# Layer 1's softmax join written one step later, V's products three steps behind the scores, and the last head's share of the output projection kept apart

## The chip, the cores and the metric

The kernel runs on one core of a Trainium2 chip. The metric is the device time of one execution in microseconds. The engines are called as in the profile: PE (TensorE, matrix products), DVE (VectorE), ACT (ScalarE), POOL (GpSimd), SP (SyncE, which here only issues DMAs).

## What is computed

The reference is a two-layer backbone over 1024 latent tokens (`x`, 1024 wide) and 256 context tokens, batch 1. Layer 0 is multi-head latent attention, layer 1 is differential attention. Both kernels compute layer 0 in the same way; the change lies in layer 1, where the context tokens serve as keys and values alone:

```python
def diff_mixer(h, h_c, rows, need_ctx, layer_idx, w_in, lam, g_sub):
    ...
    lam_full = jnp.exp(jnp.sum(lam[0] * lam[1])) - jnp.exp(jnp.sum(lam[2] * lam[3])) + lambda_init
    q, k, v, gate = project(h, True)              # 8 heads, two q/k pairs of 64 each, v of 128, rotary on q and k
    q_c, k_c, v_c, gate_c = project(h_c, False)
    o1, o1_c = prefix_attention(q[:, :, :, 0:1], k[:, :, :, 0], v, ...)   # softmax over 1024 + 256 keys
    o2, o2_c = prefix_attention(q[:, :, :, 1:2], k[:, :, :, 1], v, ...)
    o = o1 - lam_full * o2
    o = rms_norm(o, g_sub) * (1.0 - lambda_init)
    return gated(o, gate)                          # o * silu(gate)
...
x = layer_norm(DEEPNORM_ALPHA * x + gate[:, None, :] * (o @ out_w[i]), ln_g[i], ln_b[i])
```

## The kernel before

All of layer 1 is cut into steps (h, t): head h of eight, tile t of eight with 128 query tokens each. In the profile it runs from about 1020 us to the end. Products that need more than half precision are made as three matmuls of high and low halves (`mm3`, lines L187 to L189). All PSUM banks (eight of 512 floats) are taken in turn under one name, `ps_b`.

A step of head h does the following, on the engines named:

- Scores (`scores1`): PE makes the scores of tile t against 1280 keys for both softmaxes m = 0, 1 (L1147, L1148; tiles `KS`, `QS`, `Q1`), the 256 context keys of both first. DVE takes the maxima (L1160, L1164, joined in L1166, L1169; tile `mx`), ACT the six exponentials with their sums (L1172, into `p0`, `p1` and `sm`).
- Join: DVE adds the sums (L1175), takes reciprocals (L1176), forms the factor of the second softmax (L1177) and makes `p0 + factor * p1` (L1178, 128x1280). After that V needs one product instead of two.
- Turn (`turn1`): ACT rounds the joined probabilities to half precision (L1184), POOL takes the rest (L1185), SP issues a DMA that transposes both halves into `pT` (L1187).
- Values (`values1`): PE multiplies `pT` by V's halves `vh`, `vl` in 30 matmuls (L1194 to L1196), ACT scales the result (L1199) and sums its squares (L1200), POOL takes the power for the norm (`rstd_of`, L161, L162) and scales (L1207), SP stores the 128x128 tile to `o_d` in DRAM (L1208). In the last head DVE multiplies by the gate instead and writes into the output tile (L1205).

Between these pieces PE works on a second stream, the projections of the next head (`prod_k1`, `prod_q1`, `prod_v1`) and the scaled weights of the one after (`prod_w`): K and Q are projected, rotated by DVE and POOL (`rope1`, L1051 to L1054, tiles `rsw`, `kr`, `rr`), scaled and split by ACT and DVE (L183 to L184, `kH`, `kL`), and put in place by DMAs. V and the gate come out of one projection, and ACT copies them to `Vf` and `gg` (L1125, L1127). The parts of the second stream are cut into slots by the table `SLOT1` through the function `some`, which takes pieces until their cost is used up.

The values of a step are taken two steps later: `turned` holds what is waiting. Tiles come from rotating pools: `p0` and `p1` two buffers each, `pT` two, `sm` four. A tile that is taken again waits until the readers of the one before are through.

In the last head the second stream is the output projection instead. `out_open` gives the projection's memory free, loads the layer norm's rows (`gb2`, `gb3`), loads the stored output of seven heads and the gate for tile 0 (`out_load`, POOL multiplies them in L1264), and loads, scales and splits the last four of the eight weight blocks (`out_w1`, DVE, L1235 and L179). From step 2 on, step t transposes the gated output of tile t-1 (`out_turns`, PE L1276, halves `tH`, `tL` by ACT L178 and DVE L179) and multiplies tile t-2 by the weights, its last 128 columns being transposed and multiplied at the end (`out_tile1`). The layer norm follows: DVE adds and takes statistics (L1311, L1312, L1315), POOL, ACT and POOL finish (L161, L162, L1325 to L1328), SP stores. Tile 7 ends with DVE (L1320, L1321).

PE's instructions stand in the order in which the code is written. DVE, ACT, POOL and SP are put in order by a scheduler, which goes by its own costs; so a line that is written elsewhere can stand on these engines where it stood, or not.

## Time and profile before

| | |
|---|---|
| median of three runs | 1881.55 us (1880.38 to 1882.77) |
| the profiled execution | 1876.05 us, its span 1874.3 us |
| busy in the span | PE 88%, DVE 64%, ACT 56%, POOL 55% |
| mean clock granted to PE | 0.951 of full speed |
| layer 1, heads 0 to 6 | 1020 to 1691.4 us |
| layer 1, last head | 1691.4 to 1874.3 us |

The profile shows one execution. Its instructions carry the line of the kernel, the engine, the tiles by name (buffer numbers left out) and the shape; a wait names what ended it. The busy time of PE includes the fill of its array, and while PE's granted clock is below 1 its instructions take longer. In a list of waits the columns after the names are the sum in us, the count and the longest.

### The profile page before, as it was taken

The page shows a single profiled execution, that of the slowest core. Times are in us where ns is not written, and L with a number is a line of the kernel's source. Part 1 is how long each engine was busy: PE and PEld are TensorE (multiplying, and loading weights), DVE is VectorE, ACT ScalarE, POOL GpSimd, SP SyncE. Part 2 cuts the span into 40 slices and gives each one's busy share as a digit, 9 for nine tenths or more (in the row PEclk, how much of TensorE's full clock was granted, in tenths as well). Part 3 has the DMA queues.
Part 4 walks back from the last instruction along what each step waited for, and adds up shares of the span by engine and source line. Part 5 has one row for each costly group of instructions (what it writes and reads, how often), then busy time and mean ns, then how long its engine had stood idle before and what let it go on. Part 6 is the DMA issues. An engine that isn't in the chain of part 4 may idle for free. (4 is left out here: it accounts for less than half of the span.)

```text
span 1874.3 us, 35281 instructions
## 1 busy us (share of the span) xinstructions
PE 1648.6 (88%) x13828; PEld 1179.7 (63%) x13828; DVE 1192.5 (64%) x1947; ACT 1058.0 (56%) x2017; POOL 1025.5 (55%) x801
## 2 busy tenths in 40 slices
PE   7889989999999998878879988988888898883997
PEld 3889965656666665556657564756475656462766
DVE  7545765565665657436754867686867686767463
ACT  3432157877777788701124666676666676765442
POOL 1443036767777676746652546464646465665565
PEclk8999899999999999989989999999999899997999
DMA  8245630110111113053333445555454455446553
GB/s 294 73 128 185 185 106 18 39 46 23 40 44 38 29 43 110 17 202 112 112 127 111 115 105 120 116 119 121 106 112 102 107 114 111 109 86 180 147 147 98
DMA packets 277108, 196.71 MB, mean 105 GB/s; under 512 B 179303, under 2 KB 250567, under 8 KB 276942
## 3 DMA queue, kind: packets, MB, share of 16 engines
q1 hardware_dynamic: 270126, 188.17, 38.2%
q10 hardware_dynamic: 6816, 6.29, 1.0%
q8 instruction: 108, 1.77, 0.4%
q14 instruction: 58, 0.48, 0.1%
HBM read 98.65 MB, written 27.07 MB: 67 GB/s over the span
## 5 line engine op out<-in xcount | busy, mean ns | idle before, releaser
L718 POOL TENSOR_TENSOR pl<-p,ph 128x1024 f16<-128x1024 f32 (+1 forms) x176 | 363.8, 2072 | 149.0 <-ACT ph L717 122.5
L1172 ACT ACTIVATE p<-ps_b,mx 128x512 f32<-128x512 f32 (+1 forms) x384 | 231.0, 620 | 65.9 <-DVE mx L1169 53.9
L716 ACT ACTIVATE p<-ps_a,esc 128x1024 f32<-128x1024 f32 (+1 forms) x176 | 189.2, 1075 | 96.0 <-PE ps_a L774 89.5
L698 DVE TENSOR_REDUCE mx<-ps_a 128x1 f32<-128x1024 f32 x128 | 155.5, 1223 | 134.8 <-PE ps_a L696 134.8
L1185 POOL TENSOR_TENSOR p<-p,p 128x1280 f16<-128x1280 f32 x64 | 169.4, 2647 | 73.0 <-ACT p L1184 72.8
L717 ACT CAST ph<-p 128x1024 f16<-128x1024 f32 (+1 forms) x176 | 177.1, 1006 | 5.5
L1194 PE MATMUL ps_b<-vh,pT 128*128 128x128 f16 x640 | 120.8, 230 | 60.6 <-DMA pT<-p 59.9
L1164 DVE TENSOR_REDUCE mx<-ps_b 128x1 f32<-128x512 f32 x256 | 167.8, 680 | 3.2 <-PE ps_b L1148 3.1
L187 PE MATMUL ps_b<-wH,h1H 128*128 128x256 f16 x512 | 145.3, 284 | 16.5 <-ACT p L1172 16.5
L1147 PE MATMUL ps_b<-KS,QS 128*128 128x512 f16 (+1 forms) x384 | 129.0, 351 | 33.2 <-ACT p L1172 29.4
L787 PE MATMUL ps_d<-Vh,pl 128*128 128x65 f16 x1344 | 145.9, 194 | 6.7 <-POOL pl L718 6.7
L784 PE MATMUL ps_d<-Vh,ph 128*128 128x65 f16 x1344 | 148.0, 195 | 0.0
L786 PE MATMUL ps_d<-Vl,ph 128*128 128x64 f16 x1344 | 146.8, 193 | 0.0
L188 PE MATMUL ps_b<-wL,h1H 128*128 128x256 f16 x512 | 145.1, 283 | 0.0
L189 PE MATMUL ps_b<-wH,h1L 128*128 128x256 f16 x512 | 144.7, 283 | 0.0
L187 PE MATMUL ps_b<-h1H,wH 128*128 128x512 f16 (+1 forms) x384 | 135.3, 352 | 6.3 <-ACT wH L183 6.2
L189 PE MATMUL ps_b<-h1H,wL 128*128 128x512 f16 (+1 forms) x384 | 134.5, 350 | 0.7 <-DVE wL L184 0.7
L188 PE MATMUL ps_b<-h1L,wH 128*128 128x512 f16 (+1 forms) x384 | 134.9, 351 | 0.0
L784 PEld LDWEIGHTS <-ph 128*128 128x128 f16 x1344 | 123.2, 97 | 18.1 <-issue 4.8
L1184 ACT CAST p<-p 128x1280 f16<-128x1280 f32 x64 | 80.4, 1257 | 92.5 <-DVE p L1178 77.6
L1148 PE MATMUL ps_b<-KS,Q 128*128 128x512 f16 (+1 forms) x384 | 131.6, 352 | 0.0
L786 PEld LDWEIGHTS <-ph 128*128 128x128 f16 x1344 | 123.9, 98 | 12.0
(370 smaller groups left out, 5012.1 us busy)
## 6 DMA issues: line engine op xcount, KB each, us to landing
ws<-in_dw SPq DMA_DIRECT2D x30, 512.0 KB, 5.1
adw<-in_ada_w SPq DMA_DIRECT2D x24, 512.0 KB, 4.8
g<-sg_d SPq DMA_DIRECT2D x18, 512.0 KB, 3.9
adaw<-in_ada_w SPq DMA_DIRECT2D x16, 512.0 KB, 6.9
sg_d<-gg ACTq DMA_DIRECT2D x40, 128.0 KB, 3.3
o<-o_d SPq DMA_DIRECT2D x10, 512.0 KB, 3.5
o_d<-op SPq DMA_DIRECT2D x7, 640.0 KB, 3.3
xt<-in_xT SPq DMA_DIRECT2D x16, 256.0 KB, 3.6
```

The source lines that it names most:

```text
L187: pe.matmul(ps, aH, bH, start=start, stop=False, skip_group_check=skip)
L188: pe.matmul(ps, aH, bL, start=False, stop=False, skip_group_check=skip)
L189: pe.matmul(ps, aL, bH, start=False, stop=stop, skip_group_check=skip)
L698: dve.tensor_reduce(mx[:, t, 0:1], ps, axis=AX.X, op=ALU.max)
L716: act.activation(p32[:, :n], st, AF.Exp, scale=esc0)
L717: act.copy(ph[:, :n], p32[:, :n])
L718: pool.tensor_tensor(pl[:, :n], p32[:, :n], ph[:, :n], op=ALU.subtract)
L784: pe.matmul(pv[:, t, :], ph[:, ts], Vh[:, k, h, :], start=(k == kcs[0] and t == 0), stop=False, skip_group_check=True)
L786: pe.matmul(pv[:, t, :V0], ph[:, ts], Vl[:, k, h, :], start=False, stop=False, skip_group_check=True)
L1164: dve.tensor_reduce(mx[:, 2 + 2 * m + i:3 + 2 * m + i], b, axis=AX.X, op=ALU.max, negate=True)
L1172: act.activation(p[m][:, c0:c0 + n], b, AF.Exp, bias=nb, accum_out=sm[:, 2 + 3 * m + i:3 + 3 * m + i])
L1185: pool.tensor_tensor(hl[:, 1, :], p0, hl[:, 0, :], op=ALU.subtract)
```

## The change

In heads 0 to 6 the join, the rounding and the subtraction become a function `join1`, which is written in the next step, between the scores of m = 0 and the first slot. The DMA that transposes is issued at the end of that step. Values are taken three steps behind the scores (`keep` is 2), after the second slot instead of ahead of it; from step (6,7) on two steps behind. For this a third buffer `pTx` takes every third tile. It lies where `Vf` lay, and V's float copy now uses K's tile `kr`. The stores to `o_d` are put on a list `late` and issued at the end of the step.

In the last head, the output of seven heads is 896 columns wide, and the last head's share has tiles of its own (`o7`, `g7`). `out_main(t-1)` multiplies the seven blocks in step t, `out_fin(t-2)` transposes the eighth, multiplies it into banks of its own and adds them on DVE, which makes two more additions per tile. The table `FIN` says where these pieces stand between those of `out_main`. The rows of the layer norm are loaded at the end of step 1, the four weight blocks through four `z` buffers. Scores and values of the last head stand in steps 0 to 9, the table `VO` says in which slot values stand, and the stores of the output are issued a step later.

The core of the diff (the renamed parts and the tables of the tiles are cut):

```diff
+FIN = 2, 4, 7, 10
+VO = 0, 2, 0, 0, 0, 0, 0, 0, 0, 0
...
-            "Vf": ([P, NT, P], F32, 1), "cosB": ([P, SEQ], F32, 1),
+            "pTx": ([P, 2 * NT, P], F16, 1), "cosB": ([P, SEQ], F32, 1),
...
-        gg, Vf = w1("gg"), w1("Vf")
...
-            yield
+            yield p, sm
+
+    def join1(h, t, p, sm):
...
-        yield turn1(*p), sm
-
-    def turn1(p0, p1):
-
-        hl = p1.bitcast(F16).rearrange("p (a b) -> p a b", a=2)
-        act.copy(hl[:, 0, :], p0)
-        pool.tensor_tensor(hl[:, 1, :], p0, hl[:, 0, :], op=ALU.subtract)
-        pT = w1("pT")
-        sp.dma_start_transpose(pT, hl.rearrange("p a b -> p (a b)"))
-        return pT
+        hl = p[1].bitcast(F16).rearrange("p (a b) -> p a b", a=2)
+        act.copy(hl[:, 0, :], p[0])
+        pool.tensor_tensor(hl[:, 1, :], p[0], hl[:, 0, :], op=ALU.subtract)
+        nT[0] += 1
+        pT = w1("pTx" if nT[0] % 3 == 0 and (h, t) < (H1 - 2, 5) else "pT")
+        turned.append((h, t, pT, sm))
+        return lambda: sp.dma_start_transpose(pT, hl.rearrange("p a b -> p (a b)"))
...
-            dve.scalar_tensor_tensor(oo[:, c], o, ss[:, 1:2], g[:, c], op0=ALU.mult, op1=ALU.mult)
+            o7[t] = w1("o7")
+            dve.scalar_tensor_tensor(o7[t], o, ss[:, 1:2], og[t][1], op0=ALU.mult, op1=ALU.mult)
...
-        sp.dma_start(o_d[1][t * P:(t + 1) * P, h * P:(h + 1) * P], o)
...
+        late.append((step[0], lambda: sp.dma_start(o_d[1][t * P:(t + 1) * P, h * P:(h + 1) * P], o)))
...
+        rest = [big.tile([P, 5, D], F32R, tag=tg, name=nm("o1")) for tg in ("bigA", "bigB")]
+        oHL.extend([r[:, k - NOW, :] for r in rest] for k in range(NOW, KT))
+        out_load(0)
+
+    def out_ws(*ks):
+        for k in ks:
+            for _ in out_w1(k, lambda: w1("z")):
+                pass
+
+    def out_gb():
         for tag, src in (("gb2", ln_g), ("gb3", ln_b)):
             og[tag] = w1(tag)
             bcast_row(og[tag], src[1:2, :])
-        rest = [big.tile([P, 5, D], F32R, tag=tg, name=nm("o1")) for tg in ("bigA", "bigB")]
-        oHL.extend([r[:, k - NOW, :] for r in rest] for k in range(NOW, KT))
-        out_load(0)
-        for k in range(NOW, KT):
-            z = [w1("z"), w1("res")][k % 2]
-            for _ in out_w1(k, lambda: z):
-                pass
-            if k == NOW:
-                out_load(1)
...
+        o, g, g7 = w1("o"), w1("g"), w1("g7")
+        og[t] = o, g7
+        sp.dma_start(o, o_d[1][ts, :DH])
+        sp.dma_start(g, sg_d[1][ts, :DH])
+        sp.dma_start(g7, sg_d[1][ts, DH:])
+        pool.tensor_tensor(o, o, g, op=ALU.mult)
...
+    def out_main(t):
+
+        z = zs[t] = w1("z")
+        sp.dma_start(z, zn_d[t * P:(t + 1) * P, :])
+        y = [bank("b") for _ in range(2)]
+        for k0, k1 in ((0, 4), (4, KT - 1)):
+            for hh in range(2):
+                for k in range(k0, k1):
+                    out_mm(y, t, hh, k, 0, KT - 2)
+                    yield 1600
+                if k1 == KT - 1:
+                    c = slice(hh * 512, hh * 512 + 512)
+                    dve.tensor_tensor(z[:, c], y[hh], z[:, c], op=ALU.add)
+
+    def out_fin(t):
         ts = slice(t * P, (t + 1) * P)
+        out_turn(t, KT - 1, 1)
+        yield 256
+        z, bs = zs.pop(t), w1("bs")
         y = [bank("b") for _ in range(2)]
+        for hh in range(2):
+            out_mm(y, t, hh, KT - 1, KT - 1, KT - 1)
             c = slice(hh * 512, hh * 512 + 512)
+            dve.tensor_tensor(z[:, c], y[hh], z[:, c], op=ALU.add)
             dve.bn_stats(bs[:, hh, :], z[:, c])
...
+        late.append((step[0] + 1, lambda: sp.dma_start(out[ts, :], z)))
...
+        def step1(cur, side, at, vpos=1):
+
+            if cur:
+                S = scores1(*cur)
+                pq = next(S)
+            turn = None
+            keep = 2 if cur and cur < (H1 - 2, SEQ // P - 1) else 1 if joined else 0
+            if joined:
+                turn = join1(*joined.pop(0))
             some(side, at[0])
+            if cur:
+                next(S)
+                joined.append((*cur, *pq))
+            for i, v in enumerate(at[1:]):
+                if i == vpos:
+                    while len(turned) > keep:
+                        values1(*turned.pop(0))
                 some(side, v)
+            if turn:
+                turn()
+            while late and late[0][0] <= step[0]:
+                late.pop(0)[1]()
+            step[0] += 1
...
+        out_open()
+        n = SEQ // P
+        for t in range(n + 2):
+            if t == 0:
+                out_ws(4, 5)
+                G = iter(())
+            else:
+                if t == 1:
+                    out_ws(6, 7)
+                    out_load(1)
+                if t < n - 1:
+                    out_load(t + 1)
+                if t == 1:
+                    late.append((step[0], out_gb))
+                if t < n:
+                    G = weave(out_main(t - 1), chain(out_turns(t), out_fin(t - 2) if t >= 2 else ()),
+                              FIN if t >= 2 else (9, 12))
+                    if t == 1:
+                        G = chain(out_turns(0), G)
+                elif t == n:
+                    F = out_fin(t - 2)
+                    G = weave(out_main(t - 1), (v for _, v in zip(range(1), F)), (7,))
+                else:
+                    G = chain(F, out_fin(t - 2))
             credit[0] = 0
+            step1((H1 - 1, t) if t < n else None, G, SLOTO, VO[t])
```

How this moves instructions is shown at three places. The first is DVE in head 5, from the end of step 2 to step 3: L1175 to L1178 (after: L1182 to L1185) are the join of tile 2, L1160 and L1164 (after: L1164, L1168) the maxima of tile 3, L184 (L186) the low halves of K and Q, L1051 and L1052 (L1055, L1056) the rotation of Q. Before:

```order
L184 SCALAR_TENSOR_TENSOR kL_19006<-kr_18619,kc_92,kH_19005 128x1280
L1175 TENSOR_REDUCE sm_18868<-sm_18868 128x2
L1051 STREAM_SHUFFLE rsw_18981<-ps_b_18899 128x512
L1052 TENSOR_TENSOR rr_18980<-ps_b_18899,cosB_12236 128x512
L1176 RECIPROCAL sm_18868<-sm_18868 128x2
L1160 TENSOR_REDUCE mx_19025<-ps_b_19029 128x2
L1177 SCALAR_TENSOR_TENSOR sm_18868<-sm_18868,nlam 128x1
L1164 TENSOR_REDUCE mx_19025<-ps_b_19035 128x1
L1178 SCALAR_TENSOR_TENSOR p_2803_18869<-p_2804_18870,sm_18868,p_2803_18869 128x1280
L1164 TENSOR_REDUCE mx_19025<-ps_b_19054 128x1
L184 SCALAR_TENSOR_TENSOR kL_19014<-rr_18980,es_18283,kH_19013 128x512
```

The rotation, the low half of K and the first maxima stand inside the join. After:

```order
L1182 TENSOR_REDUCE sm_18819<-sm_18819 128x2
L1183 RECIPROCAL sm_18819<-sm_18819 128x2
L1184 SCALAR_TENSOR_TENSOR sm_18819<-sm_18819,nlam 128x1
L1185 SCALAR_TENSOR_TENSOR p_2798_18820<-p_2799_18821,sm_18819,p_2798_18820 128x1280
L1055 STREAM_SHUFFLE rsw_18938<-ps_b_18857 128x512
L1056 TENSOR_TENSOR rr_18937<-ps_b_18857,cosB_12236 128x512
L186 SCALAR_TENSOR_TENSOR kL_18957<-kr_18577,kc_92,kH_18956 128x1280
L1164 TENSOR_REDUCE mx_18976<-ps_b_18980 128x2
L1168 TENSOR_REDUCE mx_18976<-ps_b_18986 128x1
L1168 TENSOR_REDUCE mx_18976<-ps_b_18990 128x1
```

The four parts of the join now stand together, ahead of the rotation, the low half of K and all maxima of tile 3; the low half of Q has gone behind these.

The second place is DVE at the opening of the last head: L1235 and L179 (after: L1237, L181) scale the weight blocks (`z`, `res`) and take their low halves, L1178 (L1185) are joins, `tL` is the low half of the transposed output of tile 0, for which PE's first products of the output wait. Before:

```order
L1178 SCALAR_TENSOR_TENSOR p_3131_21065<-p_3132_21066,sm_21064,p_3131_21065 128x1280
L1235 SCALAR_TENSOR_TENSOR z_20950<-z_20950,gsub,gate_12249 128x1024
L1178 SCALAR_TENSOR_TENSOR p_3117_20981<-p_3118_20982,sm_20980,p_3117_20981 128x1280
L179 TENSOR_TENSOR o_3102_20944<-z_20950,o_3101_20943 128x1024
L1235 SCALAR_TENSOR_TENSOR res_20962<-res_20962,gsub,gate_12249 128x1024
L1166 TENSOR_SCALAR mx_21152<-mx_21152 128x1
L1164 TENSOR_REDUCE mx_21152<-ps_b_21162 128x1
L1235 SCALAR_TENSOR_TENSOR z_20967<-z_20967,gsub,gate_12249 128x1024
L179 TENSOR_TENSOR o_3102_20944<-res_20962,o_3101_20943 128x1024
L1235 SCALAR_TENSOR_TENSOR res_20974<-res_20974,gsub,gate_12249 128x1024
L179 TENSOR_TENSOR o_3102_20944<-z_20967,o_3101_20943 128x1024
```

The join of tile 1 stands ahead of that of tile 0, and the weights follow with the maxima of tile 2 between them. After:

```order
L1185 SCALAR_TENSOR_TENSOR p_3107_20952<-p_3108_20953,sm_20951,p_3107_20952 128x1280
L1237 SCALAR_TENSOR_TENSOR z_20940<-z_20940,gsub,gate_12249 128x1024
L1182 TENSOR_REDUCE sm_21059<-sm_21059 128x2
L1237 SCALAR_TENSOR_TENSOR z_20945<-z_20945,gsub,gate_12249 128x1024
L181 TENSOR_TENSOR o_3099_20932<-z_20940,o_3098_20931 128x1024
L1237 SCALAR_TENSOR_TENSOR z_21034<-z_21034,gsub,gate_12249 128x1024
L181 TENSOR_TENSOR o_3099_20932<-z_20945,o_3098_20931 128x1024
L1237 SCALAR_TENSOR_TENSOR z_21039<-z_21039,gsub,gate_12249 128x1024
L181 TENSOR_TENSOR o_3099_20932<-z_21034,o_3098_20931 128x1024
L181 TENSOR_TENSOR tL_21101<-ps_b_21102,tH_21100 128x512
L181 TENSOR_TENSOR o_3099_20932<-z_21039,o_3098_20931 128x1024
L181 TENSOR_TENSOR tL_21101<-ps_b_21109,tH_21100 128x384
```

The four scalings and three low halves now stand behind the join of tile 0 and ahead of the first `tL`; the join of tile 1 comes after both parts of `tL`.

The third place is POOL at the very end: L1327 and L1328 (after: L1341, L1342) are the layer norm's products and sums of tile 6, the powers of `mv` belong to the layer norm and those of `ss` to the attention's norm of tile 7. Before:

```order
L161 TENSOR_SCALAR mv_22323<-mv_22323 128x1
L162 TENSOR_TENSOR mv_22323<-mv_22323,neghalf 128x1
L1325 TENSOR_SCALAR mv_22323<-mv_22323 128x1
L161 TENSOR_SCALAR ss_22365<-ss_22365 128x1
L162 TENSOR_TENSOR ss_22365<-ss_22365,neghalf 128x1
L1327 TENSOR_TENSOR z_22311<-z_22311,gb_3099_20939 128x1024
L1328 TENSOR_TENSOR z_22311<-z_22311,gb_3100_20941 128x1024
L161 TENSOR_SCALAR mv_22434<-mv_22434 128x1
L162 TENSOR_TENSOR mv_22434<-mv_22434,neghalf 128x1
```

The power of tile 7's attention norm stands ahead of tile 6's products, that of its layer norm behind them, with the whole of tile 7's products on PE between the two. After:

```order
L163 TENSOR_SCALAR ss_22431<-ss_22431 128x1
L164 TENSOR_TENSOR ss_22431<-ss_22431,neghalf 128x1
L163 TENSOR_SCALAR mv_22452<-mv_22452 128x1
L164 TENSOR_TENSOR mv_22452<-mv_22452,neghalf 128x1
L1339 TENSOR_SCALAR mv_22452<-mv_22452 128x1
L1341 TENSOR_TENSOR z_22206<-z_22206,gb_3152_21219 128x1024
L163 TENSOR_SCALAR mv_22477<-mv_22477 128x1
L1342 TENSOR_TENSOR z_22206<-z_22206,gb_3153_21221 128x1024
L164 TENSOR_TENSOR mv_22477<-mv_22477,neghalf 128x1
```

Now the two norms of tile 7 stand closer to each other, and tile 6's products are between them, the last one directly ahead of the last power.

More of the change, by code (lines that the diff above doesn't have):

```diff
@@ L1241, in out_open @@
         prj.close()
+        opened.append(1)
         wo = a1.enter_context(spool("a1out"))
@@ L1398, in hybrid_kernel @@
             for _ in G:
                 pass
-        for t in range(SEQ // P - 2, SEQ // P):
-            G = weave(out_tile1(t), out_turns(t + 1), (9, 12))
+        while later:
+            later.pop(0)()
+        out_open()
[22 more added lines that the diff above has]
+                    G = chain(F, out_fin(t - 2))
```

97 lines of the change are left out of this document (24 added, 73 removed).

## The prediction

> **What bounds the kernel now.** I read the page first, then the stretches of layer 1 (heads 0 to 6 run from 1020 to 1691.4 us, the last head from there to the end), then the waits of each engine in them, then single rows. Layer 0 and the set-up run the same instructions in both kernels, so everything before 1020 us is left as it is.
>
> ```profile
> PE 1648.6 (88%) x13828; PEld 1179.7 (63%) x13828; DVE 1192.5 (64%) x1947; ACT 1058.0 (56%) x2017; POOL 1025.5 (55%) x801
> ...
> 1020.00:1691.40 671.40, 590.10 (x4730) 409.42 (x4729) 480.10 (x912) 446.78 (x1157) 363.91 (x364) 0.95 0.50 111
> 1691.40:1733.25 41.85, 12.76 (x99) 8.54 (x97) 34.27 (x42) 21.98 (x43) 22.64 (x16) 0.68 0.59 184
> 1733.25:1865.00 131.75, 125.22 (x746) 96.74 (x747) 62.89 (x131) 52.47 (x133) 75.55 (x69) 0.99 0.50 136
> ```
>
> The columns after the length are the busy times of PE, PEld, DVE, ACT and POOL, then PE's granted clock. PE is the fullest engine, and in heads 0 to 6 it stands still for 671.4 - 590.1 = 81 us. These are its waits there:
>
> ```profile
> PE ps_b L1194 <- DMA pT<-p: 34.9, 19, 3.7
> PE ps_b L1147 <- ACT p L1172: 26.1, 23, 4.6
> PE ps_b L187 <- ACT p L1172: 16.5, 6, 3.7
> ```
>
> The first is V's product waiting for the transposed probabilities, which the third pT buffer and the longer lag are made to remove. The others wait for a PSUM bank that the exponentials still read. Whether the 34.9 us are worth 34.9 us is the question, and two whole heads answer it (4, then 5, each with PE's wait for pT):
>
> ```profile
> 1404.70:1500.90 96.20, 85.40 (x685) 58.75 (x683) 68.05 (x131) 65.09 (x169) 52.93 (x54) 0.95 0.49 106
> PE ps_b L1194 <- DMA pT<-p: 0.6, 1, 0.6
> ...
> 1500.90:1593.20 92.30, 82.51 (x681) 57.66 (x679) 67.25 (x128) 62.19 (x157) 53.71 (x53) 0.96 0.53 111
> PE ps_b L1194 <- DMA pT<-p: 6.2, 3, 2.2
> ```
>
> Head 4 is nearly free of this wait and takes 96.2 us; head 5 waits 6.2 us and takes 92.3. The wait is not what makes a head long: where PE doesn't wait for pT, it waits for a bank a little later. Who waits for whom on the other side:
>
> ```profile
> DVE sm L1175 <- ACT p L1172: 112.9, 43, 3.7
> DVE mx L1160 <- PE ps_b L1148: 1.4, 3, 0.8
> ...
> ACT p L1172 <- DVE mx L1169: 53.9, 23, 4.8
> ACT p L1184 <- DVE p L1178: 49.5, 42, 3.5
> ```
>
> DVE waits 112.9 us for the exponentials (L1175 is the first instruction of the join) and 1.4 us for the context's scores; ACT waits 103.4 us for DVE. So a chain bounds the heads: maxima, six exponentials, join, the next maxima. PE follows it.
>
> **The change, part by part.** *Heads 0 to 6.* Written one step later, the join could go behind the next step's maxima and open that chain. On DVE it hardly does: in most steps the sum still stands ahead of the next step's maxima, waiting for the same six exponentials. What is left are small moves, priced by these rows of head 5 (mean ns behind the comma):
>
> ```profile
> L1164 DVE TENSOR_REDUCE mx<-ps_b 128x1 f32<-128x512 f32 x32 | 20.9, 679 | 0.0
> L1178 DVE SCALAR_TENSOR_TENSOR p<-p,sm,p 128x1280 f32<-128x1280 f32 x8 | 13.5, 1685 | 0.3
> ...
> L184 DVE SCALAR_TENSOR_TENSOR kL<-kr,kc,kH 128x1280 f16<-128x1280 f32 x1 | 1.5, 1543 | 0.0
> L184 DVE SCALAR_TENSOR_TENSOR kL<-rr,es,kH 128x512 f16<-128x512 f32 x2 | 1.5, 743 | 1.7 <-DMA Q<-kL 1.7
> L1052 DVE TENSOR_TENSOR rr<-ps_b,cosB 128x512 f32<-128x512 f32 x2 | 1.3, 672 | 0.0
> ...
> L288 DVE TENSOR_SCALAR uw<-uw 128x1 f32<-128x1 f32 x2 | 0.3, 144 | 0.0
> ```
>
> - Join 2 leaves its place behind the low half of K (1.54), the two operations of a rotation (0.67 each at least) and two maxima (1.36): it ends about 4.2 us earlier. This takes most of the pT wait of steps 4 and 5. The next maxima have the same work ahead of them as before, less one low half of Q (0.74): exponentials 3 start about 0.7 us earlier.
> - In step 4 the first three exponentials no longer have a low half of Q (0.74) and a join (1.69) ahead of them on DVE, but a maximum (0.68) moves behind the sum of step 3: up to 1.75 us earlier for three of the six, nothing for the others. I take half, 0.9.
> - In step 6 of four heads the weights' scales (six operations like L288, 0.15 each) go ahead of the maxima: 0.9 us later, 0.5 as a mean over the heads.
> - In step 5 two operations of that size move behind the maxima: 0.3 us earlier.
>
> Together -0.7 - 0.9 + 0.5 - 0.3 = -1.4 us per head, times seven: **-10 us**. The bounds are +0.9 x 7 = +6 (only the delay comes through) and -48 (first rival). PE's freed pT waits are otherwise taken over by the bank waits. The third buffer and V's float copy in `kr` add no instruction; the copies into `kr` need K's halves to be read, which ACT and DVE do two steps earlier, and K's next rotation needs vl, which stands ahead of it on DVE in both kernels. The o_d stores, now issued at a step's end, leave SP free for the transposition; nobody waits for them before the last head.
>
> *Opening of the last head.* Today PE has its longest hole here, from 1708.3 to 1733.25:
>
> ```profile
> PE ps_b L1194 <- DMA pT<-p: 24.9, 1, 24.9
> ...
> SPq L1187 <- POOL p L1185: 17.5, 1, 17.5
> ...
> 1712.06 2.67 DVE L1235 SCALAR_TENSOR_TENSOR z<-z,gsub,gate 128x1024 f32<-128x1024 f32 x1 [0.34 <-issue]
> ...
> 1716.12 1.21 DVE L179 TENSOR_TENSOR o<-z,o 128x1024 fp32r<-128x1024 f32 x1
> 1717.25 1.27 DVE L1235 SCALAR_TENSOR_TENSOR res<-res,gsub,gate 128x1024 f32<-128x1024 f32 x1
> ...
> 1719.23 3.43 DVE L1235 SCALAR_TENSOR_TENSOR z<-z,gsub,gate 128x1024 f32<-128x1024 f32 x1
> 1722.58 3.10 DVE L179 TENSOR_TENSOR o<-res,o 128x1024 fp32r<-128x1024 f32 x1
> ```
>
> SP's transposition waits 17.5 us for POOL, whose order puts tile 1 ahead of tile 0. After the change that transposition isn't the next thing PE needs: it goes to the transposes of tile 0's output and its first products. These need tL, and DVE has four scalings and three low halves of the weights ahead of tL. Starting at 1712.06, 20.7 us into the head, they take 4 x 1.27 + 3 x 1.21 = 8.7 us undisturbed and 4 x 3.43 + 3 x 3.10 = 23 at the slowest rows. The new stretch has one subtraction of POOL less beside it than today's, in which about half of the rows are slow, so I add a third of the difference, 5. PE gets on at 20.7 + 13.7 = 34 us (ends 30 and 44) where it took 41.85. The Trainium skill, "SBUF — State Buffer", section "Who interferes with whom", says that a DVE instruction with two SBUF inputs is blocked by a GpSimd instruction that reads SBUF, for its whole length; by that each of POOL's operations there (a subtraction of 2.6 us and two products of 2.1) would cost DVE its full time: an estimate of 36 us and a sum 2 us higher. The rows of 1.27 and 3.43 agree with it.
>
> *Steps of the last head.* From the hole's end to PE's end 125.2 us are busy. Of that fall away 1.3 (its clock of 0.99), tile 0's seven transposes (done before, under 1) and 3.1 (the last 12 products, now behind V's last product, 0.26 each); 2.2 (scores of tile 2) and 1.7 (V's product of (6,7)) come in from before the hole: 124 us. The prices are from these rows, the starts of the last scores, of V's product after them, of the output's first product and of the third after it:
>
> ```profile
> 1821.52 0.28 PE L1147 MATMUL ps_b<-KS,QS 128*128 128x256 f16 x1
> ...
> 1823.69 0.22 PE L1194 MATMUL ps_b<-vh,pT 128*128 128x128 f16 x1
> ...
> 1825.34 0.48 PE L187 MATMUL ps_b<-oH,tH 128*128 128x512 f32 x1
> ...
> 1826.12 0.40 PE L187 MATMUL ps_b<-oH,tH 128*128 128x512 f32 x1
> ...
> PE ps_b L187 <- ACT tH L178: 6.1, 6, 1.3
> ```
>
> The 6.1 us of waits for tH go, since tile t's products now come a step behind its transposes; the k=7 transposes behind each V product bring new ones for o7, whose norm shares POOL with the layer norm. I take 4 us, ends 0 and 14.
>
> *Tail.* Now V's last product is followed by nearly the whole norm, the last 12 products and the layer norm:
>
> ```profile
> 1854.57 0.37 ACT L1199 ACTIVATE o<-ps_b,sm 128x128 f32<-128x128 f32 x1 [3.96 <-PE ps_b L1196]
> ...
> 1855.10 0.19 POOL L161 TENSOR_SCALAR mv<-mv 128x1 f32<-128x1 f32 x1 [6.07 <-DVE mv L1315]
> ...
> 1857.23 0.35 DVE L1205 SCALAR_TENSOR_TENSOR o<-o,ss,g 128x128 f32<-128x128 f32 x1 [2.22 <-POOL ss L162]
> ...
> 1857.65 2.39 POOL L1327 TENSOR_TENSOR z<-z,gb 128x1024 f32<-128x1024 f32 x1 [0.45 <-ACT z L1326]
> ...
> 1862.39 0.27 ACT L178 CAST tH<-ps_b 128x128 fp32r<-128x128 f32 x1 [4.82 <-PE ps_b L1276]
> ...
> 1865.13 1.37 DVE L1311 TENSOR_TENSOR z<-ps_b,res 128x512 f32<-128x512 f32 x2 [2.15 <-PE ps_b L189]
> ...
> 1869.83 1.41 DVE L1321 SCALAR_TENSOR_TENSOR z<-z,mv,gb 128x512 f32<-128x512 f32 x2 [0.44 <-POOL mv L162]
> ```
>
> From ACT's copy of V's product (1854.57) to the end of the row that writes o7's place (1857.58) are 3.0 us; transpose and split, five operations of some 0.3, 1.5; three products and their drain 1.0; the first sum 0.7. Tile 6's statistics then stand on DVE ahead of tile 7's, and its two POOL products ahead of the last power: today from 1855.1 (its statistics) to the second product's end 7.4 us (1857.65 + 2 x 2.39), and the power 1. Then come one scaling (1.4) and the transfer, 3.1 from 1871.24 to the span's end. Sum 19.1, with V's own drain 20; with tile 7's power free of tile 6, 4 us less.
>
> The last head is thus 34 + 124 + 4 + 20 = 182 us against 182.9 today (1691.4 to 1874.3): **-1 us**, ends -13 (30, and no wait at all) and +20 (44, and 14). With the heads: **-11 us**. The profiled execution took 1876.05 us, 5.5 us under the median of 1881.55, so it would become 1865; against the median I forecast 1870.
>
> **Rivals.** *PE's waits are the path.* Then the 34.9 us go, and with fewer gaps the clock recovers: 590 us at 0.95 hold at most 29.5 us of lost clock, of which 34.9/81 is 13. Together -48: 1834. For it: PE is 88% busy, the fullest engine. Against: heads 4 and 5. The Trainium skill, "TensorE: Matmul & The Clock Gate", section "HAM oscillation", warns of idle gaps over some 3.4 us, after which the array runs at half rate; V's product after the hole shows the clock falling, the waits in the heads are mostly 2 us, and the rule adds weight to this rival only.
>
> *Slower.* The output's last share waits at every tile: each k=7 transpose stands on PE ahead of the next scores, and waits for o7, whose power on POOL may stand behind a 2.39 us product of the layer norm. At 2 us for seven tiles (14 instead of 4) and PE's start 38 us into the head, halfway to the slow end, the last head costs 14 us more; behind two such products, 4.8 us a tile, 34 more. I take 19 more than the sum, +8: 1889. From the sum's -11 it decides at 15 more, which is 2.7 us per tile if the start stays at 34. For it: POOL is busy 75.6 of 131.75 us there. Against: two products are 4.8 us of the some 16 us that each tile has (131.75 us for eight).
>
> *Nothing changes.* DVE's order keeps join and maxima, POOL and SP follow, the hole only moves: 1881.
>
> **How the numbers follow.** The forecast 1870 gets 0.46, its own range 1856 to 1881; the first rival 0.19, the slower one 0.22, no change 0.13. 0.2% is 3.8 us, about what a measurement of this kernel tells from none. Faster: 0.40 of the forecast's 0.46, 0.19, and 0.01 of "nothing": 0.60. Within: 0.05, 0.11 and 0.01 of the slower: 0.17. Slower: 0.23. The range leaves out the outer part of the first rival and of the slower one: 1832 to 1890.
>
> **What would show it.** PE's wait for pT between 1024 and 1690 falls under 12 us while its bank waits grow, and the heads still take 91 to 96 us; DVE's wait at the sum stays near 113. PE's longest hole begins near 1702 and ends 30 to 38 us into the last head, on DVE's tL, not on pT. Between V's last product and the end lie 18 to 22 us. It is wrong if the heads fall under 88 us (then PE was the path), or if the k=7 transposes wait over 2 us each.

## The result and the profile after

The changed kernel takes 1897.52 us (median; 1891.79 to 1899.8), the kernel before 1880.38 us on the same chip. The ratio is 1.0095 with an interval of 1.0068 to 1.0123: slower by 17 us, where I forecast 1870 and a range to 1890. The profiled execution took 1897.52 us, its span is 1895.7 us.

The engines' busy times hardly moved: PE is busy 1649.5 us where it was 1648.6, DVE 1197.3 (1192.5), ACT 1056.2 (1058.0), POOL 1045.0 (1025.5).

The stretches tell where the time went. Both kernels are cut at the first scores of layer 1 and at the first scores of the last head; after the length stand the busy times of PE, PEld, DVE, ACT and POOL, then the granted clock. First before, then after, with the last head also cut where PE gets on and where V's last product ends:

```profile
1024.40:1691.40 667.00, 585.70 (x4690) 405.49 (x4688) 478.82 (x911) 445.24 (x1154) 363.91 (x364) 0.95 0.51 111
1691.40:1874.30 182.90, 138.75 (x846) 105.59 (x844) 102.75 (x182) 74.44 (x176) 99.88 (x87) 0.90 0.50 143
```

```profile
1029.20:1708.60 679.40, 582.97 (x4690) 399.90 (x4689) 470.45 (x911) 442.02 (x1152) 386.07 (x362) 0.95 0.50 108
1708.60:1740.50 31.90, 10.15 (x66) 5.80 (x63) 26.68 (x31) 20.98 (x44) 18.41 (x14) 0.64 0.90 256
1740.50:1877.30 136.80, 126.50 (x769) 98.59 (x769) 74.06 (x151) 52.13 (x130) 72.75 (x66) 0.96 0.45 125
1877.30:1895.70 18.40, 3.84 (x17) 2.12 (x14) 10.70 (x16) 2.28 (x5) 7.46 (x9) 0.70 0.15 58
```

Heads 0 to 6 are 12.4 us longer, the last head is 31.9 + 136.8 + 18.4 = 187.1 us where it was 182.9, 4.2 longer. The other 4.8 us lie before layer 1, where both kernels have the same instructions in the same order; the profiled executions below reach layer 1 anywhere between 1019.5 and 1034.2 us, so I read stretches, not ends.

In the heads PE's wait for the transposed probabilities is gone from the list of waits after:

```profile
DVE sm L1182 <- ACT p L1176: 99.1, 44, 4.7
ACT kH L185 <- POOL rr L1058: 58.6, 13, 8.3
...
PE ps_b L1151 <- ACT p L1176: 48.3, 32, 5.7
ACT wH L185 <- DVE uw L290: 40.9, 13, 7.3
PE ps_b L189 <- ACT p L1176: 33.6, 8, 5.8
```

PE's two bank waits are 48.3 + 33.6 = 81.9 us, where they were 26.1 + 16.5 = 42.6: the 34.9 us went to them in full, as the prediction said. ACT's waits at K's and Q's high halves and at the weights' (`kH`, `wH`) have grown. Before they were:

```profile
ACT kH L183 <- POOL rr L1054: 38.7, 12, 6.4
...
ACT wH L183 <- DVE uw L288: 10.9, 6, 1.8
```

At `wH` this is mostly a shift: ACT's waits for `uw` make 40.9 us after and 45.2 before, where 19.4 of them stood at `kH` and 14.9 at the rounding. The 19.9 us more for POOL's `rr` are new, and they point at the place. Cut from join to join, one interval stands out: from join 2 to join 3 a head takes 14.5 us before and 19.2 after (mean of heads 1 to 5); the other seven together are 2 us shorter. Part of this is only join 2's own earlier place, which the change itself brings: from join 1 to join 4 a head takes 37.8 us before and 40.9 after, so some 3 us are really lost there. This is head 5, before: joins and the last maximum of tile 3 on DVE, subtraction and rotation sum on POOL, the last exponential of tile 2, high half of Q, squares of the weights and the first exponential of tile 3 on ACT.

```profile
1535.09 0.49 ACT L1172 ACTIVATE p<-ps_b,mx 128x256 f32<-128x256 f32 x1
...
1539.05 2.63 DVE L1178 SCALAR_TENSOR_TENSOR p<-p,sm,p 128x1280 f32<-128x1280 f32 x1
...
1539.07 1.26 POOL L1054 TENSOR_TENSOR rr<-rr,rsw 128x512 f32<-128x512 f32 x1
...
1540.37 0.72 ACT L183 ACTIVATE kH<-rr,es 128x512 f16<-128x512 f32 x1 [4.00 <-POOL rr L1054]
...
1543.05 2.62 POOL L1185 TENSOR_TENSOR p<-p,p 128x1280 f16<-128x1280 f32 x1 [1.32 <-ACT p L1184]
...
1543.58 1.04 ACT L981 ACTIVATE wH<-ws 128x1024 bf16<-128x1024 f32 x1
...
1544.42 0.20 DVE L1169 TENSOR_SCALAR mx<-mx,lcf 128x1 f32<-128x1 f32 x1
...
1544.62 0.67 ACT L1172 ACTIVATE p<-ps_b,mx 128x512 f32<-128x512 f32 x1
...
1552.47 1.54 DVE L1178 SCALAR_TENSOR_TENSOR p<-p,sm,p 128x1280 f32<-128x1280 f32 x1
```

And after:

```profile
1546.49 0.49 ACT L1176 ACTIVATE p<-ps_b,mx 128x256 f32<-128x256 f32 x1
...
1547.75 1.55 DVE L1185 SCALAR_TENSOR_TENSOR p<-p,sm,p 128x1280 f32<-128x1280 f32 x1
...
1553.07 2.61 POOL L1188 TENSOR_TENSOR p<-p,p 128x1280 f16<-128x1280 f32 x1
...
1555.20 0.27 DVE L1170 TENSOR_SCALAR mx<-mx 128x1 f32<-128x1 f32 x1
...
1555.64 1.26 POOL L1058 TENSOR_TENSOR rr<-rr,rsw 128x512 f32<-128x512 f32 x1
...
1556.93 0.72 ACT L185 ACTIVATE kH<-rr,es 128x512 f16<-128x512 f32 x1 [6.34 <-POOL rr L1058]
...
1557.56 1.04 ACT L984 ACTIVATE wH<-ws 128x1024 bf16<-128x1024 f32 x1
...
1558.60 0.67 ACT L1176 ACTIVATE p<-ps_b,mx 128x512 f32<-128x512 f32 x1
...
1568.02 1.66 DVE L1185 SCALAR_TENSOR_TENSOR p<-p,sm,p 128x1280 f32<-128x1280 f32 x1
```

POOL now has the subtraction of join 2 ahead of the rotation's sum, ACT waits 6.34 us for that sum in front of the exponentials, and these begin 3.1 us after the last maximum was there (1555.47). From join 2 to the first exponential of tile 3 (exponential 3 for short) pass 10.85 us, where it was 5.57. Join 2 has moved, so the fairer measure is from the end of the last exponential 2: the last maximum is there after 9.04 us before and 8.49 after, the first exponential 3 starts after 9.04 before and 11.62 after.

The lines that do this are not in the core of the diff that I showed: the change also drops a wrapper in `step1`, three times, around scores, join and values. `HP` is 0, and I took the wrapper for one without effect:

```diff
-            with tc.high_priority(HP):
-                if cur:
-                    S = scores1(*cur)
-                    next(S)
+            if cur:
+                S = scores1(*cur)
+                pq = next(S)
```

### The profile page after: what moved, and what is told of

Its sections match the earlier page's. It is cut to its first block, busy times and chain, and to the rows that moved or that the text cites. A ratio compares the mean times of both kernels' runs of the same rounds, so it can differ in the third digit from the quotient of the medians.

```text
span 1895.7 us, 35367 instructions
## 1 busy us (share of the span) xinstructions
PE 1649.5 (87%) x13828; PEld 1175.3 (62%) x13828; DVE 1197.3 (63%) x1963; ACT 1056.2 (56%) x2017; POOL 1045.0 (55%) x801
## 4 chain that ended last, share of the span: by engine, by line
PE 36%; DVE 22%; ACT 15%; POOL 13%; DMA 7%; issue 6%; SPq 1%; POOLq 0%; ACTq 0%; DVEq 0%
ACT p L1176 7%; PE ps_a L774 3%; PE ps_b L191 3%; DVE mx L1168 3%; PE ps_a L775 3%; PE ps_a L776 3%; PE ps_b L189 3%; PE ps_b L190 3%; PE ps_a L698 2%; PE ps_a L189 2%; PE ps_a L191 2%; PE ps_a L190 2%; ACT p L718 2%; POOL p L1188 2%; DVE p L1185 2%
## 5 line engine op out<-in xcount | busy, mean ns | idle before, releaser
L719 ACT CAST ph<-p 128x1024 f16<-128x1024 f32 (+1 forms) x176 | 177.1, 1006 | 5.4
L189 PE MATMUL ps_b<-wH,h1H 128*128 128x256 f16 x512 | 144.3, 282 | 35.9 <-ACT p L1176 33.6
L1168 DVE TENSOR_REDUCE mx<-ps_b 128x1 f32<-128x512 f32 x256 | 166.4, 679 | 0.2
L189 PE MATMUL ps_b<-h1H,wH 128*128 128x512 f16 (+1 forms) x384 | 135.6, 353 | 10.8 <-ACT wH L185 6.2
L788 PEld LDWEIGHTS <-ph 128*128 128x128 f16 x1344 | 124.9, 99 | 12.4 <-issue 0.8
L774 PE MATMUL ps_a<-qH,KH 100*128 100x512 f16 x320 | 123.2, 385 | 9.2 <-ACT p L718 4.3
L789 PEld LDWEIGHTS <-pl 128*128 128x128 f16 x1344 | 124.1, 98 | 6.6 <-POOL pl L720 6.5
```

The costliest lines, as they stand in the source:

```text
L189: pe.matmul(ps, aH, bH, start=start, stop=False, skip_group_check=skip)
L774: pe.matmul(s_, kh[:nr, ks], QH[:nr, :], start=True, stop=False)
L788: pe.matmul(pv[:, t, :V0], ph[:, ts], Vl[:, k, h, :], start=False, stop=False, skip_group_check=True)
L789: pe.matmul(pv[:, t, :], pl[:, ts], Vh[:, k, h, :], start=False, stop=(k == NT - 1), skip_group_check=True)
L1168: dve.tensor_reduce(mx[:, 2 + 2 * m + i:3 + 2 * m + i], b, axis=AX.X, op=ALU.max, negate=True)
```

## The experiments

Heads and last head are cut as above, from one profiled execution each; the next column is the interval from join 2 to join 3 (mean of heads 1 to 5); the ratio is to the kernel before on the same chip. The expectations count the heads up to the last join, 1 to 2 us less. The ratios don't add up with the two stretches to the microsecond: e5 lies 31.6 us under the changed kernel by the ratios and 23.8 by the stretches, e7 15.0 and 8.6. I rest the cause on the stretches.

| kernel | heads 0-6 | last head | join 2 to 3 | median us | ratio |
|---|---|---|---|---|---|
| before | 667.0 | 182.9 | 14.5 | 1880.38 | 1 |
| after | 679.4 | 187.1 | 19.2 | 1897.52 | 1.0095 (1.0068 to 1.0123) |
| e0 before, no wrapper in heads 0-6 | 680.6 | 182.9 | 18.5 | 1890.69 | 1.0056 (1.0035 to 1.0076) |
| e1 after's heads, before's last head | 679.8 | 183.9 | 19.2 | 1893.91 | 1.0075 (1.0044 to 1.0106) |
| e2 before's heads, after's last head | 667.5 | 172.9 | 14.2 | 1868.26 | 0.9940 (0.9913 to 0.9967) |
| e3 after, wrapper everywhere | 661.1 | 185.5 | 9.4 | 1876.36 | 0.9977 (0.9954 to 1.0000) |
| e4 after, rotation's sum on DVE | 696.6 | 187.2 | 22.4 | 1910.60 | 1.0170 (1.0144 to 1.0195) |
| e5 after, wrapper in heads 0-6 and two steps of the last | 664.3 | 178.4 | 10.0 | 1865.11 | 0.9927 (0.9906 to 0.9949) |
| e6 as e5, layer norm ends on DVE | 664.5 | 167.7 | 9.9 | 1859.16 | 0.9899 (0.9869 to 0.9928) |
| e7 after, wrapper in two steps of the last head | 679.0 | 178.9 | 19.2 | 1881.69 | 1.0015 (0.9995 to 1.0035) |
| e9 after, wrapper in step 2 of heads 0-6 | 660.8 | 186.4 | 8.7 | 1875.88 | 0.9998 (0.9977 to 1.0019) |
| e10 after, wrapper as e5 but for the steps 2 | 678.8 | 178.4 | 19.4 | 1879.17 | 1.0014 (0.9994 to 1.0034) |
| e11 as e5, V two steps behind | 663.8 | 177.1 | 9.3 | 1871.80 | 0.9974 (0.9951 to 0.9996) |
| e12 as e6, wrapper in step 2 and two steps of the last | 660.6 | 169.1 | 8.4 | 1855.64 | 0.9889 (0.9861 to 0.9917) |

**The wrapper alone (e0).** In the kernel before, the edit is

```diff
-            with tc.high_priority(HP):
+            high = lambda: nullcontext() if cur and cur[0] < H1 - 1 else tc.high_priority(HP)
+            with high():
```

at its three places.

> The kernel before, with one thing taken away: the three priority scopes around scores, join and values in the steps of heads 0 to 6 (the changed kernel has dropped them; their argument is 0). Join, lag, buffers and the last head stay as before. Theory A (the dropped scopes made the heads longer: without them POOL takes the subtraction of tile 2 ahead of the sum that ends Q's rotation, and ACT puts Q's high half ahead of the exponentials of tile 3): join 2 to join 3 grows from 13.4-15.4 to 17-20 us, the kernel to about 1892 us, 10 to 15 more than before. Rival B (the later join, the lag or the shared tile made the heads longer, the scopes do nothing): within 4 us of before, about 1880.

The heads go from 667.0 to 680.6 us with nothing of the join, the lag or the buffers changed, and the interval from join 2 to join 3 goes from 14.5 to 18.5. So an offset of 0 is not without effect, and the loss in the heads comes without the change's other parts. Why the scheduler orders otherwise with it isn't shown.

**The two halves (e1, e2).** e1 keeps all of the change in heads 0 to 6 and has the last head of before behind it; e2 has the heads of before, wrapper and two `pT` buffers included, and the last head after.

> Heads 0 to 6 as in the changed kernel (no scopes, join a step later, lag three, third buffer, stores at the step's end), the last head as before. Both theories put the larger part of the loss into the heads: about +12 us against before, 1892. If the loss were the last head's alone: 1880.

> Heads 0 to 6 as before with their scopes, the last head as in the changed kernel. From the two profiles the last head itself costs 4 to 5 us more (187.1 us from its first scores against 182.9), so about 1885; if the last head had been a gain that the heads' loss hid: 1875 or less.

e1 has the whole loss of the heads (679.8). e2 shows that the last head kept apart is a gain: 172.9 us where before takes 182.9. That it is 5.5 us less than e5's, which has the same last head behind later joins, is for the most part PE's clock: from its first product with `tL` to V's last product PE is busy 123.8 us in e2 and 128.4 in e5, at a mean granted clock of 0.98 and 0.95.

**The wrapper put back (e3, e5, e7).** They differ in the condition under which the wrapper stands around the three places:

```diff
+ e3:  with tc.high_priority(HP):
+ e5:  high = lambda: tc.high_priority(HP) if cur and cur < (7, 2) else nullcontext()
+ e7:  high = lambda: tc.high_priority(HP) if cur and (7, 0) <= cur < (7, 2) else nullcontext()
```

> The changed kernel with the scopes put back around scores, join and values in all steps. Theory A: join 2 to join 3 falls from 19-20 us to 14 or less, the heads are 12 us or more shorter, the kernel 1880 to 1885. With the first exponentials of tile 3 now ahead of the rounding of tile 2 on ACT the heads could even come out shorter than before: 1875. Rival B: unchanged, about 1897.

> The changed kernel with the scopes put back in heads 0 to 6 and in the first two steps of the last head, and left out after that: the heads of e3_scope (659 us) and a last head that opens with the first low half of the transposed output behind one weight scaling, and whose later steps are those of e2_last (171.7 us from the join of (6,7) to the end). If the parts add up: e3_scope's 1876 less 12.7, about 1864, 15 less than before. If instead the last head's gain in e2_last came from the state in which it is entered (lag two), it stays near 1876.

> The changed kernel with the scopes in the first two steps of the last head alone; heads 0 to 6 without them. This puts the first low half of the transposed output ahead of three of the four weight scalings on DVE. If that place is what the opening costs: PE's wait of 10.8 us falls to 2 to 3, and the kernel from 1897 to about 1886. If something else holds PE there: no change, 1897.

With the wrapper the heads of the changed kernel take 661 to 664 us, 3 to 6 less than before. In the first two steps of the last head it is worth 8.2 us (187.1 to 178.9, e7); in all of its steps it costs 7.1 (178.4 to 185.5, e5 against e3). PE's wait for `tL` falls from 10.8 to 3.75 us in e7 (2 to 3 were expected). e5 is faster than before.

**The rotation's sum on DVE (e4).** If the sum is late because it stands behind POOL's subtraction, it could be made elsewhere:

```diff
-        pool.tensor_tensor(r[:, :n], r[:, :n], sw[:, :n], op=ALU.add)
+        dve.tensor_tensor(r[:, :n], r[:, :n], sw[:, :n], op=ALU.add)
```

> The changed kernel, still without scopes; the sum that ends a rotation (the last line of rope1) is taken from POOL and given to DVE, 0.67 us each. Theory A, in its mechanism: what makes join 2 to join 3 long is that on POOL this sum stands behind the subtraction of tile 2, Q's high half on ACT waits for it, and the exponentials of tile 3 wait behind that. Then the interval falls from 19.2 us (mean of heads 1 to 5) to 16 or less though DVE has more to do, and the kernel from 1897 to 1875-1885. Rival: ACT's own order alone does it (Q's half and a weight's half ahead of the exponentials, 1.7 us of work); then the interval stays above 18 and the kernel gets no faster than 1893.

The interval grew to 22.4. The rows of head 5:

```profile
1565.07 3.86 POOL L1188 TENSOR_TENSOR p<-p,p 128x1280 f16<-128x1280 f32 x1
...
1566.38 3.09 DVE L1058 TENSOR_TENSOR rr<-rr,rsw 128x512 f32<-128x512 f32 x1
```

DVE's sum ends at 1569.47, 0.54 us after POOL's subtraction (1568.93): it was held up by it all the same, and now the maxima stand behind it too. By the letter the rival's signs came (over 18 us, not under 1893), but the test adds a cost of its own and decides between neither.

**Step 2 alone, and all but step 2 (e9, e10).** The wrapper's condition once more:

```diff
+ e9:  if cur and cur[0] < H1 - 1 and cur[1] == 2
+ e10: if cur and cur < (H1 - 1, 2) and cur[1] != 2
```

> The changed kernel with the raised priority put back in one step of each of heads 0 to 6 only, t = 2 (its scores, the join of t = 1 and V's product), nowhere else. Theory A (what the changed kernel loses in the heads is the order of step 2 into step 3: POOL's subtraction ahead of the rotation's sum, and ACT's high half of Q and squares of the weights ahead of exponentials 3): this alone brings the heads from 677.3 back to 661-666 us, the interval from join 2 to join 3 from 19.2 to about 10; the last head stays at 183-187; time 1897.5 - 13 = 1884 (1880-1888). Theory B (the scopes work all over the step, each step a little): an eighth of the gain, heads 674-677, join 2 to 3 over 16, time 1893-1897.

> The opposite: the changed kernel with the raised priority in all steps of heads 0 to 6 but t = 2, and in the first two of the last head. Theory A: heads stay at 675-679 us, join 2 to 3 near 19, the last head is 177-178 as with the scopes in its opening alone; time 1881 (1878-1885), as that kernel. Theory B: heads 662-668, join 2 to 3 under 13, time 1868-1873.

```profile
1034.20:1695.00 660.80, 577.41 (x4690) 398.57 (x4688) 481.74 (x911) 442.24 (x1152) 376.31 (x362) 0.96 0.52 111
```

That row is e9's heads. One step in eight brings the whole 18.6 us (679.4 to 660.8), the seven others bring none of it (678.8, e10). From join 1 to join 4 a head takes 37.5 us in e9 and 40.9 in e10; of the 10.5 us by which the interval from join 2 to join 3 falls, 7.1 are a shift, for the intervals beside it grow by as much. By the expectations e9's heads are 658.8 us, 2 less than its range, and e10's 676.7. e9's median came out 4 us under its range; its ratio lies 0.0097 under that of the changed kernel, 18 us, which is the heads. Head 5 of e9 at the place:

```profile
1543.39 0.67 ACT L1176 ACTIVATE p<-ps_b,mx 128x512 f32<-128x512 f32 x1
```

```profile
1542.79 1.54 DVE L1185 SCALAR_TENSOR_TENSOR p<-p,sm,p 128x1280 f32<-128x1280 f32 x1
...
1550.39 2.64 DVE L1185 SCALAR_TENSOR_TENSOR p<-p,sm,p 128x1280 f32<-128x1280 f32 x1
```

The first exponential 3 runs 0.6 us after join 2 begins, and join 3 follows in 7.6 us: here the later join opens the chain, as the prediction said that it could and "on DVE it hardly does".

**The lag (e11).** Three steps or two, all else as e5:

```diff
-                keep = 2 if cur and cur < (H1 - 2, SEQ // P - 1) else 1 if joined else 0
+                keep = 1 if cur and cur < (H1 - 2, SEQ // P - 1) else 1 if joined else 0
```

> The changed kernel with the scopes in heads 0 to 6 and the first two steps of the last head (1865.11), and V's products two steps behind the scores instead of three, the join still written one step later. Theory A (PE's wait for the transposed probabilities is not the path in the heads, the bank waits take it over): PE's waits for pT come back, at 20-40 us between 1024 and 1690, its bank waits shrink by as much, heads 660-666 us (662.3), time 1863-1869. Theory C (the longer lag is what the scoped kernel gains from): heads 670-690, time over 1872.

```profile
PE ps_b L1151 <- ACT p L1176: 28.3, 26, 3.6
PE ps_b L189 <- ACT p L1176: 27.0, 8, 5.0
PE ps_b L1198 <- DMA pT<-p: 14.8, 10, 2.8
PE ps_b L1198 <- DMA pTx<-p: 9.5, 3, 7.5
```

The waits for the transposed tiles are back (24.3 us with those for the third buffer), the bank waits fall from 77.2 in e5 to 55.3, and heads (663.8 against 664.3) and last head (177.1 against 178.4) stay. The median is 3 us over its range and the ratio 0.0047 above e5's; in the profiles the two differ only before layer 1 (first scores at 1031.1 and 1019.5). Whether the lag is worth something that these profiles don't show is open.

**Layer norm on DVE (e6), and both (e12).** Tiles 0 to 6 end with the four DVE instructions of tile 7 instead of ACT's and POOL's, with one store per tile as before:

```diff
-        if t == SEQ // P - 1:
+        if True:
```

> e5_both with the layer norm of tiles 0 to 6 on DVE as tile 7 has it (four scalings of 0.7 us), instead of ACT and POOL (two products of 2.4 us). If the transposes of the eighth block wait for POOL's products ahead of the power (10 us in all in the changed kernel, and 4 us in the tail): 8 to 12 us less than e5_both, 1854. If DVE becomes the one that is late: not faster than e5_both.

> A version meant to be faster than all: the kernel with tiles 0 to 6 finished by DVE like tile 7 (1859.16), with the scopes of heads 0 to 6 cut down to t = 2, so that the join of (5,7) isn't put behind the maxima of (6,0) by them. Theory A: heads 655-662 us (8 us of head 5 come back at most, 662.4 if not), the last head 167; time 1851-1859. Theory B (scopes act in all steps): heads over 668, time over 1865.

e6's last head is 10.7 us shorter than e5's. From PE's first product with `tL` to V's last product the two are, e5 first:

```profile
1703.50:1843.70 140.20, 128.37 (x770) 100.14 (x770) 86.95 (x158) 56.60 (x136) 81.58 (x69) 0.95 0.54 146
```

```profile
1711.10:1843.40 132.30, 123.78 (x770) 97.03 (x769) 102.21 (x182) 49.13 (x130) 55.84 (x51) 0.98 0.56 154
```

Of the 10.7 us, 4.6 are PE's busy time at a higher granted clock, 3.3 are waits (the 3.00 us before the transpose of the eighth block of tile 6 above all), 2.4 lie behind V's last product and 0.3 in the opening. Waits of 0.6 to 1.5 us at five of these transposes remain: the power for o7 is now ready 2 us or more before o7 starts, but o7 stands on DVE behind the maxima.

e12 has the lowest median of all, 1.1% under the kernel before, with an interval that overlaps e6's; head 5, from which 8 us were to come back, gave 2 (103.4 to 101.4 us from the last join of head 4 to that of head 5, before 95.4).

## Why the prediction was wrong

**Heads 0 to 6: -10 predicted, +12.4 measured.** The step that failed is "exponentials 3 start about 0.7 us earlier": it let them follow DVE's maxima and priced DVE's order alone. The dropped wrapper moved POOL's and ACT's order as well, was in neither the sum nor the rivals, and I costed it at nothing without naming what it might reorder. e0, e9 and e10 show that it is the cause and step 2 the place.

The first half of that step held. Counted from the end of the last exponential 2, in heads 1 to 5, the last maximum 3 is there after 9.0 to 12.3 us before and 8.5 after. What came later is POOL's sum for Q: it ends after 4.75 us before and 9.9 to 10.9 after. `kH` and `wH` stand behind it on ACT, and the exponentials, which began with the last maximum before (9.0 to 12.2 us), now begin behind these two (11.6 to 12.6). e0 has the same picture (maximum 9.5, sum 9.7, exponential 12.1). In head 5 the sum's 5.2 us are 1.9 for DVE's rotation, which stands behind the join, 0.2 until POOL takes it up, 1.2 for POOL's product of the rotation (2.44 us instead of 1.27, beside a low half of K on DVE) and 2.0 for the subtraction, where a scaling of 0.6 stood. These are readings of rows: the wrapper moves all the orders at once, e4 failed to part them, and no run shows what one of them would be worth alone.

With the wrapper the rest of the change gains 3 (e5) to 6 us (e3), less than the 10.

**"PE follows" was right.** The pT wait fell to nothing and the bank waits took it over. In the changed kernel the longer heads blur this; e5 shows it best, with bank waits of 77.2 us where the two and the pT wait were 77.5 before, and heads 2.7 us shorter, and e11 shows it in the other direction. The first rival (1834) is out: 34.9 us of wait were removed and almost no time with them. The other two signs fail: heads of 93 to 102 us (from last join to last join) where I wrote 91 to 96, and DVE's wait at the sum 99.1 (103.8 over the heads' own stretch) where I wrote 113; why it shrank isn't shown.

**Opening: 34 predicted, 31.9 measured**, on tL, as said. PE's row after:

```profile
1740.48 0.80 PE L191 MATMUL ps_b<-oH,tL 128*128 128x512 f32 x1 [10.80 <-DVE tL L181]
```

And DVE's scalings in front of tL:

```profile
1725.02 1.82 DVE L1237 SCALAR_TENSOR_TENSOR z<-z,gsub,gate 128x1024 f32<-128x1024 f32 x1 [2.73 <-DMA z<-in_out_w]
...
1726.83 3.57 DVE L1237 SCALAR_TENSOR_TENSOR z<-z,gsub,gate 128x1024 f32<-128x1024 f32 x1
...
1731.46 3.09 DVE L1237 SCALAR_TENSOR_TENSOR z<-z,gsub,gate 128x1024 f32<-128x1024 f32 x1
...
1735.61 3.08 DVE L1237 SCALAR_TENSOR_TENSOR z<-z,gsub,gate 128x1024 f32<-128x1024 f32 x1
...
1739.75 0.68 DVE L181 TENSOR_TENSOR tL<-ps_b,tH 128x512 fp32r<-128x512 f32 x1
```

They begin 16.4 us into the head (I took 20.7) and take 14.7 us to tL (I took 13.7). With the wrapper in these steps tL stands behind one scaling: PE waits 3.75 us for a later part of it (e7). No term of mine asked whether that order was the only one.

**Steps: 124 + 4 predicted, 136.8 measured.** Busy are 126.5; the rest is waits. The term of 4 us was too small: the k=7 transposes (of the eighth block) wait 10.2 us up to V's last product, on the mechanism of the "Slower" rival. One of them:

```profile
1777.21 2.39 POOL L1341 TENSOR_TENSOR z<-z,gb 128x1024 f32<-128x1024 f32 x1 [1.36 <-ACT z L1340]
...
1779.68 2.38 POOL L1342 TENSOR_TENSOR z<-z,gb 128x1024 f32<-128x1024 f32 x1
...
1782.42 0.55 POOL L164 TENSOR_TENSOR ss<-ss,neghalf 128x1 f32<-128x1 f32 x1
```

```profile
1783.01 0.35 DVE L1208 SCALAR_TENSOR_TENSOR o<-o,ss,g 128x128 f32<-128x128 f32 x1 [7.56 <-POOL ss L164]
```

```profile
1783.50 0.30 PE L1282 MATMUL ps_b<-idr,o 128*128 128x128 f32 x1 [2.33 <-DVE sm L1182]
```

The power for o7 stands behind both products, o7 comes 7.56 us after DVE was free for it, PE waits 2.33 (the row names DVE's next instruction as releaser; o7 ends at 1783.36). At all six tiles with such a wait the power ends behind the second product. With these products taken from POOL the longest wait (3.00 us, tile 6) is gone and the sum falls from 8.2 us in e5 to 5.1 in e6: the rival's mechanism is shown. But less than a third of e6's 10.7 us are these waits. At about 1.5 us a tile the waits did not reach the 2.7 at which the prediction lets this rival decide.

**Tail: 20 predicted, 18.4 measured**, inside 18 to 22; with tile 6's products off POOL it is 16.0 (e6), for the 4 us less that I named.

The last head is 187.1 us for 182: 2.1 less at the opening, 2.5 more busy time, 6.3 more waits, 1.6 less at the end. That it is only 5 us off is luck in part: misses of both signs offset each other. The ends -13 and +20 that I gave for it don't follow from the terms beside them, which make -9 and +19; -13 needs the 4 us of the tail as well.

## What to carry to other kernels

Where a scheduler sets the order, every line that the change drops belongs into the sum, wrappers with an offset of zero too: compare the order on each engine with that one line alone undone, and look at the engines beside the one you are pricing. A wait that a change takes away was worth almost nothing here, where the next wait is for the same chain. An interval between two points of a step that grew (here join 2 to join 3) found the place faster than a list of waits did, but measure the loss between points that the change doesn't move. Ask which of several inputs comes last: the maxima that I priced came earlier and no longer counted. A short instruction that the matrix engine waits for (here the power of o7) shouldn't share a queue with long ones that nobody waits for, nor should what follows it on another engine (here o7 behind the maxima in e6).

## What the hardware showed beside it

Three scalings on DVE that began beside an instruction of POOL ended 1.1 us after it, whatever its length. POOL's rows there:

```profile
1725.71 3.61 POOL L1188 TENSOR_TENSOR p<-p,p 128x1280 f16<-128x1280 f32 x1
...
1731.24 2.23 POOL L1270 TENSOR_TENSOR o<-o,g 128x896 f32<-128x896 f32 x1 [1.92 <-DMA g<-sg_d]
...
1734.55 3.06 POOL L1270 TENSOR_TENSOR o<-o,g 128x896 f32<-128x896 f32 x1 [1.09 <-DMA g<-sg_d]
```

These end at 1729.32, 1733.47 and 1737.61, the scalings of 3.57, 3.09 and 3.08 us at 1730.40, 1734.55 and 1738.69: each waited for POOL's end and then ran about as long as one undisturbed (1.27). In the prediction I took a third of this effect, by counting slow rows; it goes by what POOL has running at that moment. The other way round, POOL's last product (3.06 us, where one undisturbed takes 2.08) began 0.08 us after a low half on DVE (1734.47), and that one took its usual 1.21. The Trainium skill, "SBUF — State Buffer", section "Who interferes with whom", says that a DVE instruction with two inputs in SBUF contends with a POOL instruction that reads SBUF, over ports that one holds at a time; the trace agrees.

PE's clock fell after a wait of 3.00 us for the transpose of tile 6, when V's last product was still to come. In e2, after a wait of 2.99 us at the same place, it did not. After's row first, then e2's:

```profile
1868.60:1874.50 5.90, 5.88 (x15) 4.63 (x16) 0.98 (x2) 0.27 (x1) 0.00 (x0) 0.50 0.20 82
```

```profile
1845.30:1851.30 6.00, 6.00 (x50) 5.08 (x51) 1.68 (x3) 0.27 (x1) 0.00 (x0) 1.00 0.19 78
```

For 5.9 us it was 0.50 in the changed kernel. In e5 and e7 the same wait (3.00 and 2.99) is followed by a mean of 0.72 over 6 us; in e6, which hasn't got it, the clock stays at 1.00 there. After the wait of 2.33 us above it stayed at 1.00, but in e5 it fell to a mean of 0.52 over the 3.5 us behind a wait of 2.17. So the length of the one wait doesn't decide here, and what does isn't shown. The Trainium skill, "TensorE: Matmul & The Clock Gate", section "HAM oscillation", speaks of gaps over some 3.4 us; here shorter ones were enough in some runs. Half of 5.9 us is 2.9, about the 2.5 us of busy time that the steps have more than predicted; that is an estimate. It fits that e2 and e6, without this fall, are busy 123.8 us in these steps, where I predicted 124.
